# Winograd convolution on one core: the store of image 10 is cut into three transfers, two of them over 100 and 28 channels

## The chip, the cores and the metric

The kernel runs on one NeuronCore of a Trainium2 chip. The core has five engines: PE (TensorE, matrix multiply), DVE (VectorE), ACT (ScalarE), POOL (GpSimd) and SP (SyncE, which here only issues transfers). Data moves between device memory (HBM) and the on-chip memory (SBUF) by 16 DMA engines, which all queues share. A transfer is issued by an engine's queue: SP's transfers appear in the profile as queue q1, ACT's as q10, POOL's as q0; q8 and q14 carry the program's own instructions. A packet is one contiguous piece that one DMA engine moves.

The metric is device time in microseconds (us) of one execution. Three runs of the kernel before took 126.14, 126.81 and 127.47 us; the median is 126.81 us.

## What is computed

A 3x3 convolution with a border of zeros: 16 images of 64 channels and 64x64 pixels, 128 output channels, all float32.

```
for b, co, ci, kh, kw:
    output[b, co] += weight[co, ci, kh, kw] * x_pad[b, ci, kh:kh+h, kw:kw+w]
```

The input is 16.8 MB (1 MB an image), the output 33.6 MB (2 MB an image).

## The kernel before

Two images make a pair (`NP = 8` pairs, index `p` from 0 to 7), because 64 channels of two images fill the 128 partitions of SBUF. The convolution is done as a one-dimensional Winograd transform over rows: two neighbouring output rows share a product. For a block of 16 output rows (`blk` 0 to 3), `group` (L114 to L149) runs three sets of matmuls into PSUM: `U` on the sum of two input rows (`ss`), `A` for the even output rows, `Bt` for the odd ones. ACT copies `U` to SBUF (`ut`, L155), and DVE adds it to `A` (L164) and to `Bt` (L167), which leaves the finished rows in `ot`, one tile of 128 output channels (the partitions) by 64 rows by 64 columns for each image. A channel of an image is 16 KB, contiguous in SBUF and in HBM.

Input comes in three ways. The weights and the first two pairs are loaded by SP as float32 (L42, L46, L48); pairs 2 to 7 are loaded by POOL with a cast to float16 (`load`, L58). POOL also adds up the row sums `ss` of later pairs (L67).

Output is what the change touches. `store` (L96 to L100) issues one transfer of the rows `lo` to `hi` of all 128 channels. After the last block of a pair, SP stores the first image of the pair (L171), as soon as DVE's last addition to it is done; the second image is put into the list `held`, and ACT issues it in the next block, after its `ut` copies (L160 to L161). For pairs 0 to 6 a store is a whole image, 2 MB; in pair 7 each image is stored as two halves of 32 rows (L168). The tiles of images 10 to 15 (pairs 5 to 7) are not used again, so nothing in the program waits for their stores but the program's end (L200, SP).

There is one more order that the change touches. Transfers from SP and ACT take the semaphores that tell of their landing in turn, from eight: the ninth such transfer has the semaphore of the first, and its queue waits until the first has landed before it issues the ninth. In the order of the program, these transfers are the weights (1), the three loads (2 to 4), and the stores of pair 0 (5 and 6), and so on to the four stores of pair 7 (19 to 22). The store of image 10, which the change cuts, is number 15.

Of the kernel before, what the change touches and what calls it, by code (L numbers as in the profile page):

```python
# [13 lines left out]
def kernel(  # L14
# [6 lines left out]
    nc = tc.nc  # L21
    B, CI, H, W = x.shape
    CO = weight.shape[0]
    assert H == 64 and W == 64 and CI == 64 and CO == 128 and B % 2 == 0
    NP = B // 2
# [4 lines left out]
    out_rows = out.rearrange("b co h w -> b co h w")  # L30
# [25 lines left out]
    def load(p):  # L56
        xs[p] = xpool.tile([128, H, W], F16, tag="xs", name="xs")
        keep(nc.gpsimd.dma_start(xs[p], x_rows[128 * p : 128 * p + 128, :, :]))  # L58
# [3 lines left out]
    def sums(eng, p, src, lo, n):  # L62
        if p not in ss:
            ss[p] = spool.tile([128, H // 2, W], F16, tag="ss", name="ss")
        v = src.rearrange("p (j i) c -> p j i c", i=2)
        keep(
            eng.tensor_add(  # L67
                ss[p][:, lo : lo + n, :], v[:, lo : lo + n, 0, :], v[:, lo : lo + n, 1, :]
            )
        )  # L70
# [22 lines left out]

    held = []

    def store(eng, p, b2, ot, lo, hi):  # L96
        return eng.dma_start(
            out_rows[2 * p + b2, :, lo:hi, :],
            ot.rearrange("p j i c -> p (j i) c")[:, lo:hi, :],
        )  # L100

    for p in range(NP):
        if p + 1 < NP:
            for lo in (0, 16):
                sums(nc.gpsimd, p + 1, x1 if p == 0 else xs[p + 1], lo, 16)
        if p > 0 and p + 4 < NP:
            load(p + 4)
        ots = [
            opool.tile([128, H // 2, 2, W], F32, tag="ot", name="ot") for _ in range(2)
        ]  # L110
        for blk in range(4):
            j0 = blk * RB

            def group(wi_rows):  # L114

                tiles = [
                    psum.tile([128, RB, W], F32, tag="acc", name="acc") for _ in range(2)
                ]
                n = 3 * len(wi_rows)
                i = 0  # L120
                for wi, off in wi_rows:
                    for kw in (1, 0, 2):
                        c_lo, c_hi = max(0, 1 - kw), min(W, W + 1 - kw)
                        for b2 in range(2):
                            p0 = 64 * b2
                            lo, hi = j0, j0 + RB
                            if off is None:
                                rhs = ss[p][p0 : p0 + 64, lo:hi, c_lo + kw - 1 : c_hi + kw - 1]
                            else:
                                while 2 * lo + off < 0:  # L130
                                    lo += 1
                                while 2 * (hi - 1) + off > H - 1:
                                    hi -= 1
                                first = 2 * lo + off
                                last = 2 * (hi - 1) + off
                                rhs = xs[p][
                                    p0 : p0 + 64,
                                    first : last + 1 : 2,
                                    c_lo + kw - 1 : c_hi + kw - 1,
                                ]  # L140
                            nc.tensor.matmul(  # L141
                                tiles[b2][:, lo - j0 : hi - j0, c_lo:c_hi],
                                Wt[p0 : p0 + 64, wi, kw, :],
                                rhs,
                                start=i == 0,
                                stop=i == n - 1,
                            )
                        i += 1
                return tiles  # L149

            U = group([(G1, None)])
            us = []
            for b2 in range(2):
                ut = upool.tile([128, RB, W], F32, tag="ut", name="ut")
                keep(nc.scalar.copy(ut, U[b2]))  # L155
                us.append(ut)
            if p == 0:
                for lo in {2: (0, 16), 3: (32, 48)}.get(blk, ()):
                    keep(nc.scalar.copy(xs[1][:, lo : lo + 16, :], x1[:, lo : lo + 16, :]))  # L159
            while held:  # L160
                keep(store(nc.scalar, *held.pop(0)))  # L161
            A = group([(G21, 1), (G0, -1)])
            for b2 in range(2):
                nc.vector.tensor_add(ots[b2][:, j0 : j0 + RB, 0, :], A[b2], us[b2])  # L164
            Bt = group([(G01, 0), (G2, 2)])
            for b2 in range(2):
                nc.vector.tensor_add(ots[b2][:, j0 : j0 + RB, 1, :], Bt[b2], us[b2])  # L167
            parts = {3: (0, 64)} if p < NP - 1 else {1: (0, 32), 3: (32, 64)}  # L168
            if blk in parts:
                lo, hi = parts[blk]  # L170
                store(nc.sync, p, 0, ots[0], lo, hi)  # L171
                held.append((p, 1, ots[1], lo, hi))
    while held:
        keep(store(nc.scalar, *held.pop(0)))
# [30 lines left out]
```

## Time and profile before

| what | value |
|---|---|
| median of three runs | 126.81 us |
| the profiled execution's own time | 126.72 us |
| its span, first to last instruction | 124.9 us |
| mean granted clock of PE | 0.968 |
| busy: PE, DVE, ACT, POOL | 106.7, 82.6, 44.4, 36.9 us |
| moved by DMA | 44.48 MB in 4042 packets, mean 356 GB/s |
| store of 2 MB, from issue to landing (SP, ACT) | 20.1, 19.8 us |
| issue of one store on SP | 0.33 us |

The span is what the profile covers; 1.8 us of the execution's time lie outside it. "Busy" is the time in which an engine executes, added up. The DMA share of a stretch is the mean over the 16 DMA engines, so that 1.00 means that all sixteen move data all the time; it is counted where a packet begins, so a short stretch can show more than 1.00. "From issue to landing" contains the time that a transfer stands behind others in the queues.

### The profile page before, as it was taken

The page shows a single profiled execution, that of the slowest core. Times are in us where ns is not written, and L with a number is a line of the kernel's source. Part 1 is how long each engine was busy: PE and PEld are TensorE (multiplying, and loading weights), DVE is VectorE, ACT ScalarE, POOL GpSimd, SP SyncE. Part 2 cuts the span into 40 slices and gives each one's busy share as a digit, 9 for nine tenths or more (in the row PEclk, how much of TensorE's full clock was granted, in tenths as well). Part 3 has the DMA queues.
Part 4 walks back from the last instruction along what each step waited for, and adds up shares of the span by engine and source line. Part 5 has one row for each costly group of instructions (what it writes and reads, how often), then busy time and mean ns, then how long its engine had stood idle before and what let it go on. Part 6 is the DMA issues. An engine that isn't in the chain of part 4 may idle for free.

```text
span 124.9 us, 2407 instructions
## 1 busy us (share of the span) xinstructions
PE 106.7 (85%) x978; PEld 55.9 (45%) x978; DVE 82.6 (66%) x132; ACT 44.4 (36%) x76; POOL 36.9 (30%) x29
## 2 busy tenths in 40 slices
PE   0489999999999999999999999999999999990000
PEld 0334455555555555555555555555555555540000
DVE  0106897877787778788788878777877787772000
ACT  4439569633333333333333333333333333330000
POOL 2391059997059001760008500093000000000000
PEclk9999999999999999999999999999999999999755
DMA  4999999999999999999999999999999999999991
GB/s 127 341 429 409 289 220 220 210 254 357 386 344 354 328 375 359 367 338 344 386 359 354 338 344 401 428 435 441 414 430 430 425 420 435 435 420 407 430 391 66
DMA packets 4042, 44.48 MB, mean 356 GB/s; under 512 B 448, under 2 KB 448, under 8 KB 704
## 3 DMA queue, kind: packets, MB, share of 16 engines
q1 hardware_dynamic: 1872, 21.27, 41.2%
q10 hardware_dynamic: 1296, 16.78, 31.7%
q0 software_dynamic: 864, 6.29, 24.4%
q8 instruction: 7, 0.11, 0.3%
q14 instruction: 3, 0.02, 0.0%
HBM read 17.07 MB, written 33.55 MB: 405 GB/s over the span
## 4 chain that ended last, share of the span: by engine, by line
PE 78%; DMA 6%; ACT 3%; DVE 1%; SPq 1%; issue 1%; DVEq 0%
PE acc L141 78%; DMA x<-in_x_dram 6%; ACT xs L92 2%; ACT ut L155 1%; DVE ot L164 1%; DVE ot L167 0%; DVEq L200 0%; SPq L46 0%; SPq L42 0%; DVEq L164 0%
## 5 line engine op out<-in xcount | busy, mean ns | idle before, releaser
L141 PE MATMUL acc<-xs,Wt 64*128 64x504 f16 (+3 forms) x768 | 94.8, 378 | 0.2
L141 PEld LDWEIGHTS <-Wt 64*128 64x128 f16 x960 | 54.7, 96 | 51.6 <-issue 4.2
L155 ACT COPY ut<-acc 128x512 f32<-128x512 f32 x64 | 34.3, 589 | 60.3 <-issue 40.6
L164 DVE TENSOR_TENSOR ot<-acc,ut 128x512 f32<-128x512 f32 x64 | 41.2, 686 | 21.9 <-PE acc L141 18.0
L167 DVE TENSOR_TENSOR ot<-acc,ut 128x512 f32<-128x512 f32 x64 | 41.1, 684 | 0.0
L141 PE MATMUL acc<-ss,Wt 64*128 64x504 f16 (+1 forms) x192 | 32.5, 384 | 1.0 <-DVE ss L67 1.0
L67 POOL TENSOR_TENSOR ss<-xs 128x1024 f16<-128x1024 f16 x12 | 25.2, 2126 | 23.6 <-DMA xs<-in_x_dram 12.5
L67 DVE TENSOR_TENSOR ss<-x 128x512 f16<-128x512 f32 x4 | 2.6, 689 | 8.8 <-DMA x<-in_x_dram 8.8
L58 POOL DMA_DIRECT2D xs<-in_x_dram x6 | 3.5, 578 | 13.3 <-PE acc L141 13.3
L67 POOL TENSOR_TENSOR ss<-x 128x1024 f16<-128x1024 f32 x2 | 4.7, 2360 | 7.1 <-DMA x<-in_x_dram 7.1
L84 PE MATMUL wp<-ident,w 128*64 128x128 f16 x18 | 1.3, 328 | 4.3 <-POOL w L52 4.3
L92 ACT CAST xs<-x 128x1024 f16<-128x1024 f32 (+2 forms) x4 | 4.0, 1048 | 2.3 <-DMA x<-in_x_dram 2.3
L159 ACT CAST xs<-x 128x1024 f16<-128x1024 f32 x4 | 4.0, 1058 | 0.0
L84 PEld LDWEIGHTS <-w 128*64 128x64 f16 x18 | 1.1, 210 | 4.2 <-POOL w L52 4.2
L85 ACT CAST Wt<-wp 128x384 f16<-128x384 f32 x3 | 1.2, 487 | 2.9 <-PE wp L84 2.9
L86 POOL TENSOR_TENSOR Wt<-Wt 128x384 f16<-128x384 f16 x1 | 1.5, 1460 | 1.7 <-ACT Wt L85 1.7
L85 ACT ACT_TABLE_LOAD x1 | 1.3, 1283 | 0.7 <-PEq L189 0.7
L52 POOL CAST w<-w_raw 128x576 f16<-128x576 f32 x1 | 0.7, 663 | 2.2 <-DMA w_raw<-in_weight_dram 2.2
L87 POOL TENSOR_TENSOR Wt<-Wt 128x384 f16<-128x384 f16 x1 | 0.9, 902 | 0.0
masks.py:199 POOL TENSOR_SCALAR_AFFINE_SELECT ident<-ident 128x128 f16<-128x128 f16 x1 | 0.3, 292 | 0.1
masks.py:197 POOL MEMSET ident<- 128x128 f16 x1 | 0.2, 205 | 0.3 <-POOLq L189 0.3
L189 POOL MEMSET const-float32-0.0<- 128x1 f32 x1 | 0.1, 98 | 0.2 <-issue 0.2
(3 smaller groups left out, 0.3 us busy)
## 6 DMA issues: line engine op xcount, KB each, us to landing
out_dram<-ot SPq DMA_DIRECT2D x7, 2048.0 KB, 20.1
out_dram<-ot ACTq DMA_DIRECT2D x7, 2048.0 KB, 19.8
xs<-in_x_dram POOLq DMA_DIRECT2D x6, 1024.0 KB, 25.9
x<-in_x_dram SPq DMA_DIRECT2D x1, 2048.0 KB, 14.8
out_dram<-ot SPq DMA_DIRECT2D x2, 1024.0 KB, 11.6
out_dram<-ot ACTq DMA_DIRECT2D x2, 1024.0 KB, 11.5
x<-in_x_dram SPq DMA_DIRECT2D x1, 1472.0 KB, 7.9
x<-in_x_dram SPq DMA_DIRECT2D x1, 576.0 KB, 4.7
```

The costliest lines, as they stand in the source:

```text
L58: keep(nc.gpsimd.dma_start(xs[p], x_rows[128 * p : 128 * p + 128, :, :]))
L67: eng.tensor_add(ss[p][:, lo : lo + n, :], v[:, lo : lo + n, 0, :], v[:, lo : lo + n, 1, :])
L84: nc.tensor.matmul(wp[q : q + 64, k * CO : k * CO + CO], w16[:, t::9], ident)
L85: keep(nc.scalar.copy(wrow(g), wp[:, 0 : 3 * CO]))
L86: keep(nc.gpsimd.tensor_sub(wrow(G21), wrow(G2), wrow(G1)))
L87: keep(nc.gpsimd.tensor_sub(wrow(G01), wrow(G0), wrow(G1)))
L92: keep(nc.scalar.copy(xs[0][:, lo:hi, :], x0[:, lo:hi, :]))
L141: nc.tensor.matmul(tiles[b2][:, lo - j0 : hi - j0, c_lo:c_hi], Wt[p0 : p0 + 64, wi, kw, :], rhs, start=i == 0, stop=i == n - 1,)
L155: keep(nc.scalar.copy(ut, U[b2]))
L159: keep(nc.scalar.copy(xs[1][:, lo : lo + 16, :], x1[:, lo : lo + 16, :]))
L164: nc.vector.tensor_add(ots[b2][:, j0 : j0 + RB, 0, :], A[b2], us[b2])
L167: nc.vector.tensor_add(ots[b2][:, j0 : j0 + RB, 1, :], Bt[b2], us[b2])
```

## The change

For `p == NP - 3`, which is pair 5, the store of the first image (image 10) is issued as three transfers on SP in place of one. The first takes rows 0 to 53 of all 128 channels. The second takes rows 54 to 63 of channels 0 to 99, the third the same rows of channels 100 to 127. Together they write the same bytes. The stores of the other images, the second image of pair 5 among them, stay as they are. `store` gets two more arguments, the bounds of the channels.

```diff
-    def store(eng, p, b2, ot, lo, hi):
+    def store(eng, p, b2, ot, lo, hi, c_lo=0, c_hi=CO):
         return eng.dma_start(
-            out_rows[2 * p + b2, :, lo:hi, :],
-            ot.rearrange("p j i c -> p (j i) c")[:, lo:hi, :],
+            out_rows[2 * p + b2, c_lo:c_hi, lo:hi, :],
+            ot.rearrange("p j i c -> p (j i) c")[c_lo:c_hi, lo:hi, :],
         )
...
             if blk in parts:
                 lo, hi = parts[blk]
-                store(nc.sync, p, 0, ots[0], lo, hi)
+                if p == NP - 3:
+                    store(nc.sync, p, 0, ots[0], lo, 54)
+                    store(nc.sync, p, 0, ots[0], 54, hi, 0, 100)
+                    store(nc.sync, p, 0, ots[0], 54, hi, 100, CO)
+                else:
+                    store(nc.sync, p, 0, ots[0], lo, hi)
                 held.append((p, 1, ots[1], lo, hi))
```

## Prediction

> **What bounds the kernel now.** I first read the table of DMA queues, because PE at 85% of the span leaves room for another bound.
>
> ```profile
> q1 hardware_dynamic: 1872, 21.27, 41.2%
> q10 hardware_dynamic: 1296, 16.78, 31.7%
> q0 software_dynamic: 864, 6.29, 24.4%
> q8 instruction: 7, 0.11, 0.3%
> ```
>
> The last column is each queue's time as a share of sixteen engines' span. The sum is 97.6% of 124.9 us: on average each DMA engine moves data for 121.9 us. The rest is the start (the first transfer is issued at 0.73 us) and the end. DMA is the bound, more than PE. The table also shows how a store is dealt out: q10 carries ACT's nine stores, and 1296 / 9 = 144 packets = 16 x (8 + 1): eight channels and one semaphore write for each of 16 engines.
>
> Next, stretches of the span, with the DMA share and GB/s in the last two columns.
>
> ```profile
> 12.50:75.00 62.50, 62.31 (x583) 32.66 (x581) 49.95 (x80) 25.66 (x46) 27.31 (x15) 1.00 1.02 326
> 75.00:113.00 38.00, 37.16 (x349) 19.39 (x343) 29.75 (x48) 12.16 (x23) 4.20 (x2) 1.00 1.01 426
> 113.00:121.00 8.00, 0.00 (x0) 0.00 (x0) 0.34 (x1) 0.00 (x0) 0.00 (x0) 0.75 1.00 424
> 121.00:124.90 3.90, 0.00 (x0) 0.00 (x0) 0.00 (x0) 0.00 (x0) 0.00 (x0) 0.50 0.27 113
> ```
>
> From 12.5 to 121 us all sixteen engines are full; after 113 us nothing computes. So what one engine has to do more or less in the middle is still there at its end. The waits of SP's queue agree: it waits for DVE before each store, and at the end 10.6 us for stores.
>
> ```profile
> SPq L97 <- DVE ot L167: 107.0, 9, 20.6
> SPq L200 <- DMA out_dram<-ot: 10.6, 6, 4.2
> ```
>
> The end itself, in quarters of a microsecond:
>
> ```profile
> 121.00:121.25 0.25, 0.00 (x0) 0.00 (x0) 0.00 (x0) 0.00 (x0) 0.00 (x0) 0.50 0.78 328
> 121.50:121.75 0.25, 0.00 (x0) 0.00 (x0) 0.00 (x0) 0.00 (x0) 0.00 (x0) 0.50 0.55 229
> ...
> 122.25:122.50 0.25, 0.00 (x0) 0.00 (x0) 0.00 (x0) 0.00 (x0) 0.00 (x0) 0.50 0.40 164
> 122.50:122.75 0.25, 0.00 (x0) 0.00 (x0) 0.00 (x0) 0.00 (x0) 0.00 (x0) 0.50 0.32 131
> 122.75:123.00 0.25, 0.00 (x0) 0.00 (x0) 0.00 (x0) 0.00 (x0) 0.00 (x0) 0.50 0.09 33
> 123.00:123.25 0.25, 0.00 (x0) 0.00 (x0) 0.00 (x0) 0.00 (x0) 0.00 (x0) 0.50 0.16 66
> 123.25:123.50 0.25, 0.00 (x0) 0.00 (x0) 0.00 (x0) 0.00 (x0) 0.00 (x0) 0.50 0.00 0
> ```
>
> The engines don't end together. 66 GB/s for 0.25 us are two packets of 8 KB: two engines are still at work after 123 us, while others stopped before 121.5. The packet records give each engine's end, since in the full stretch a packet begins 3 or 4 ns before the one ahead of it on its engine ends, and so the packets link into sixteen chains. They end (us) at 120.9, 121.2, 121.2, 121.3, 121.4, 121.6, 121.7; then 122.4, 122.6, 122.6, 122.7, 122.8, 122.8, 122.9; then 123.3 and 123.5. The seven instruction packets of q8 (0.88 to 0.96 us each, and some 0.4 us on the packet behind) lie in seven different chains, all of the later nine. The last chain has none; between 77 and 114 us its 16 KB packets take 0.63 to 0.66 us, where the others' take 0.61. **The program ends when the slowest of sixteen DMA engines ends.** The trace doesn't number the engines.
>
> **The change, part by part.** *Packets.* In the full stretch a 16,384 B packet takes 611 ns and an 8,192 B one 309 ns: 8192 / 302 = 27.1 B/ns and 7 ns fixed. So 54 rows (13,824 B) take 517 ns and ten rows (2,560 B) 101 ns. A semaphore write takes 9 ns. Before, image 10 costs each engine 8 x 611 + 9 = 4,897 ns.
>
> *How 100 and 28 channels are dealt out* no row shows, since every transfer here has 128. One bound is sixteen even shares, as in all rows: 8 x (517 + 101) + 27 = 4,971, +0.07 us on each engine. The far bound is one engine for both pieces: 128 x 101 = 12.9 us on it, some +12 us. Nearest to the rows, where each engine has the same whole number of channels, is the largest number of engines up to 16 that divides the channels: 10 engines with 10 channels, and 14 engines with 2. I take that, with the ten among the fourteen. Then:
> - ten engines: 8 x 517 + 12 x 101 + 27 = 5,375, **+0.48 us**
> - four engines: 8 x 517 + 2 x 101 + 18 = 4,356, **-0.54 us**
> - two engines: 8 x 517 + 9 = 4,145, **-0.75 us**
>
> The Trainium skill ("DMA: Bandwidth & Descriptors", in the section on why a DMA increments its semaphore by 16 and not by 1) gives the same division, 100 partitions on 10 engines, the lowest-numbered ones; no run here shows it yet. The same page's rules for kernel authors speak against the change: to use all 16 engines, the outermost dimension should be a multiple of 16, which 100 and 28 are not.
>
> *Does the shift reach the end?* An engine must not run dry behind it. Image 10's store is issued at 87.16 us and lands at 104.1; the next store on the queue comes at 99.97 and lands at 113.6, the one after at 106.3. Work is always queued, so each engine's end moves by its own sum.
>
> *Issues.* SP issues two more transfers.
>
> ```profile
> L97 SPq DMA_DIRECT2D out_dram<-ot x9: 332/333/348, 23.1 to 112.8; - x9
> L97 SPq EVENT_SEMAPHORE  x7: 17/17/17, 36.3 to 106.7; - x7
> ```
>
> That is 2 x 0.33 us and two semaphore waits of 17 ns, on SP at 87.5 us, with nothing queued behind until 99.97: nothing. ACT's store of image 11 (87.76 us) may overlap SP's third issue; if it had to wait out 0.33 us, ACT's next `ut` copy, which comes after some 2 us of idle time, hides it, and the DMA engines are full anyway.
>
> *Semaphores.* The eight are taken in turn, and the two new transfers (16 and 17) push each later one two places on. Number 16 needs number 8 (landed 58.0 us), 17 needs 9 (72.5), 18 needs 10 (72.7); pair 6 needs 11 and 12 (84.8), the first half of pair 7 needs 13 and 14 (94.7). The last two stores (issued at 112.8 and 113.4) now need parts of image 10, which land near 104.6: 8 us to spare. No wait binds. At the end SP waits for the semaphores in fixed order, about 60 ns a step. Before, the last landing (123.95 us) is followed by two more steps; after, the last store has the last semaphore of that order. **-0.12 us**.
>
> *The sum* depends on where the latest engines fall. Without a number on the chains, the last one is among the ten with a chance of 10/16: +0.48 - 0.12 = **+0.36 us**. On the profiled execution's 126.72 (124.9 span and 1.8 around it) that is 127.08; it lies 0.09 under the runs' median of 126.81, so 127.2 on that. I say 127.1.
>
> The skill's same page (section on latency and other measured facts) says that engines 7 and 15 are usually the slow ones, by its guess from descriptor traffic of POOL's transfers. Here one engine is slow from 77 us on, when POOL's last load is nearly done (it lands at 81.0), until 114, so the guess doesn't fit, but the numbers may: were it 7, the sum is the one above, were it 15, that engine ends at 122.7 and another is last.
>
> **Rivals.** All are counted at the 85% that I give to the 10-and-14 division, unless said.
> - *The last engine is among the six, the second last among the ten* (6/16 x 10/15): 123.32 + 0.48 = 123.80 against 123.47, +0.33 - 0.12 = +0.21: 126.9 us. Speaking for it: 0.15 us alone part the two.
> - *Both are among the six* (6/16 x 5/15): then an engine with an instruction packet is last, 122.9 + 0.48 = 123.38, -0.09 - 0.12 = -0.2: 126.5 us, faster. It can't be much more: the lightest of the nine late engines ends at 122.4, at least three of the nine are among the ten, so the end is at least 122.6 + 0.48 = 123.1, -0.5 with the semaphores: 126.2 us.
> - *The change doesn't shift load* (sixteen even shares or nearly): +0.07 - 0.12, 126.7 us, no change. For it: every row of the trace is even.
> - *The spread is narrower*, for example a power of two that divides both 100 and 28, which is four engines: 8 x 517 + 32 x 101 + 27 = 7,395, +2.5 us on four and -0.75 on the others. It costs over 1% as soon as one of the four ended after 122.2 before, as nine of sixteen did (1 - (7x6x5x4)/(16x15x14x13) = 98%): about 122.9 + 2.5 = 125.4, +1.8: 128.6 us, slower. Against it: nothing in the trace uses fewer than 16.
> - *Faster by over 1%* would need more than an even finish of all engines. The mean of the sixteen ends is 122.1; 123.47 less this is 1.4 us, 1.1%, and only three sizes of shift are to be had.
>
> **How the numbers follow.** 1%, about what a measurement here can tell from no change, is 1.27 us. Chances: last engine among the ten 0.53; second last 0.21; both among the six 0.11; no shift 0.07; narrower spread 0.06; faster for a cause I don't see 0.02. The first four lie between -0.5 and +0.4 us, within 1%. The runs before scatter by 0.7 us around their median, so a small true shift can pass 1% either way; I move 0.04 to slower, where most of it points, and 0.03 to faster. Faster 0.05, same 0.85, slower 0.10. For the range I take the cases' 126.5 to 127.2 and add half a microsecond of scatter: 126.0 to 127.7; the narrow spread stays outside.
>
> **What will show it.** q1 should have 1872 - 144 + 144 + 110 + 42 = 2024 packets (data and semaphores; 2032 if all sixteen engines take part in each piece, 2008 if four do), and in the quarter-microsecond stretches the end should show ten engines later and six earlier. The last packet begins near 123.6 us where it began at 123.15. Wrong would be: a store after 99 us issued later than DVE releases it (a semaphore wait), a DMA share under 0.95 between 90 and 120 us, or a slow engine that is another one in each execution, which would make the chances mere averages over runs.

## The result, and the profile after

The changed kernel takes 127.16 us (median of 22 runs), the one before 126.66 us (22 runs beside them). The ratio is 1.0035, with a 95% interval of 1.0019 to 1.0050: a little slower, by the ratio +0.44 us (0.24 to 0.63). The forecast was no change beyond 1%, with +0.36 us as the likeliest sum.

The profiled execution of after took 127.14 us with a span of 125.4 us. Its page, the table of DMA queues (packets, MB, share of sixteen engines' span):

```profile
q1 hardware_dynamic: 2024, 21.27, 41.1%
q10 hardware_dynamic: 1296, 16.78, 31.5%
q0 software_dynamic: 864, 6.29, 24.3%
q8 instruction: 7, 0.11, 0.3%
```

q1 moves the same bytes in 2024 packets, the number that goes with ten engines for 100 channels and fourteen for 28. Long stretches of after, with DMA share and GB/s at the end of a line:

```profile
75.00:113.00 38.00, 37.24 (x350) 31.90 (x345) 29.72 (x49) 12.35 (x24) 4.21 (x2) 1.00 1.01 426
113.00:121.00 8.00, 0.00 (x0) 0.00 (x0) 0.53 (x1) 0.00 (x0) 0.00 (x0) 0.62 1.00 424
121.00:125.40 4.40, 0.00 (x0) 0.00 (x0) 0.00 (x0) 0.00 (x0) 0.00 (x0) 0.50 0.25 102
```

From 75 to 121 us the DMA engines are as full as before, with the same GB/s. The weight loads of PE (PEld, the second busy time of a line, 31.90 us) appear longer than before (19.39), but e3 below has 19.49 and is slower still, so that is not where time goes. The difference lies in the last line, which is half a microsecond longer. In quarters of a microsecond, after:

```profile
121.50:121.75 0.25, 0.00 (x0) 0.00 (x0) 0.00 (x0) 0.00 (x0) 0.00 (x0) 0.50 0.86 361
...
122.00:122.25 0.25, 0.00 (x0) 0.00 (x0) 0.00 (x0) 0.00 (x0) 0.00 (x0) 0.50 0.24 98
122.25:122.50 0.25, 0.00 (x0) 0.00 (x0) 0.00 (x0) 0.00 (x0) 0.00 (x0) 0.50 0.23 98
122.50:122.75 0.25, 0.00 (x0) 0.00 (x0) 0.00 (x0) 0.00 (x0) 0.00 (x0) 0.50 0.31 131
122.75:123.00 0.25, 0.00 (x0) 0.00 (x0) 0.00 (x0) 0.00 (x0) 0.00 (x0) 0.50 0.08 33
123.00:123.25 0.25, 0.00 (x0) 0.00 (x0) 0.00 (x0) 0.00 (x0) 0.00 (x0) 0.50 0.08 33
123.25:123.50 0.25, 0.00 (x0) 0.00 (x0) 0.00 (x0) 0.00 (x0) 0.00 (x0) 0.50 0.08 33
123.50:123.75 0.25, 0.00 (x0) 0.00 (x0) 0.00 (x0) 0.00 (x0) 0.00 (x0) 0.50 0.00 0
```

At 121.50 more engines are at work than before (0.86 against 0.55): those that ended early now end later. From 122.75 on, one packet begins in a quarter: a single engine, which ends 0.8 us later than any other.

The packet records, linked end to start as in the prediction, show which. In after each chain also tells its class, by its packets of 2,560 B: 12, 2 or none.

```
                    ends before (us)                          ends after (us)
ten (12 packets)    not told apart                            121.5 121.7 121.8 121.9 121.9 122.1
                                                              122.6 122.8 123.0 | slow one: 123.8
four (2 packets)                                              122.0 122.1 122.1 122.8
two (none)                                                    120.7 121.9
all                 120.9 121.2 121.2 121.3 121.4 121.6 121.7
                    122.4 122.6 122.6 122.7 122.8 122.8 122.9
                    123.3 | slow one: 123.5
```

The slow engine, known by 49 packets of 16 KB at 0.63 us or more between 76 and 113 us, has 12 small packets. It is one of the ten, and it ends 0.35 us later than before. Its packets of image 10 take 5,687 ns in place of 5,204: +0.48 us, the shift that the sum has for one of the ten. Its chain was 0.07 us ahead at 83 us already, and its other packets took 0.05 us less.

The waits of SP's queue in after:

```profile
SPq L97 <- DVE ot L167: 104.9, 9, 20.8
SPq L205 <- DMA out_dram<-ot: 10.4, 3, 4.7
```

Every store still waits for DVE alone; no wait for a semaphore's earlier transfer has come in.

### The profile page after: what moved, and what is told of

Read it like the earlier page. It is cut to its first block, busy times and chain, and to the rows that moved or that the text cites. A ratio compares the mean times of both kernels' runs of the same rounds, so it can differ in the third digit from the quotient of the medians.

```text
span 125.4 us, 2409 instructions
## 1 busy us (share of the span) xinstructions
PE 106.9 (85%) x978; PEld 89.4 (71%) x978; DVE 82.7 (66%) x132; ACT 44.4 (35%) x76; POOL 36.8 (29%) x29
## 3 DMA queue, kind: packets, MB, share of 16 engines
q1 hardware_dynamic: 2024, 21.27, 41.1%
## 4 chain that ended last, share of the span: by engine, by line
PE 83%; DMA 4%; DVE 2%; issue 1%; DVEq 0%; SPq 0%
PE acc L141 83%; DMA x<-in_x_dram 4%; DVE ot L164 1%; DVE ss L67 1%; DVE ot L167 0%; DVEq L205 0%; SPq L42 0%
## 5 line engine op out<-in xcount | busy, mean ns | idle before, releaser
L141 PEld LDWEIGHTS <-Wt 64*128 64x128 f16 x960 | 88.2, 96 | 18.0 <-issue 4.2
L141 PE MATMUL acc<-xs,Wt 64*128 64x504 f16 (+3 forms) x768 | 92.0, 380 | 0.0
L141 PE MATMUL acc<-ss,Wt 64*128 64x504 f16 (+1 forms) x192 | 29.3, 384 | 1.0 <-DVE ss L67 1.0
```

The source lines that it names most:

```text
L141: nc.tensor.matmul(tiles[b2][:, lo - j0 : hi - j0, c_lo:c_hi], Wt[p0 : p0 + 64, wi, kw, :], rhs, start=i == 0, stop=i == n - 1,)
```

## Experiments

Each is an edit of the changed kernel, in the three calls of `store` for pair 5, and still writes the whole output. The times beside them are of the kernel before on the same chip.

### e1: cut in rows alone

```diff
-                    store(nc.sync, p, 0, ots[0], 54, hi, 0, 100)
-                    store(nc.sync, p, 0, ots[0], 54, hi, 100, CO)
+                    store(nc.sync, p, 0, ots[0], 54, 64)
```

> Image 10 in two transfers, rows 0 to 53 and rows 54 to 63, both of all 128 channels: cut in rows, not in channels. Theory (the slowest DMA engine ends the program and the 100 and 28 channels load ten engines more): each engine has the same share, 8 x (516 + 102) + 18 = 4962 ns against 4897, +0.07 us; the last store has the seventh of the eight semaphores in SP's final order, one step of 0.06 us less: together 0.0 us, 126.7 us. Rival (cutting the store and issuing more transfers costs the time, whatever the channels): half or more of the change's +0.5 us, 126.9 to 127.2 us.

Measured: 126.64 us (12 runs), before 126.64 (23 runs); ratio 0.9997 (0.9981 to 1.0013), between -0.24 and +0.16 us. Cutting the store in rows costs nothing that can be measured, and packets of 2,560 B alone don't either; what is left is the cut in channels. SP's stores in e1 (min/median/max duration in ns) show that a long issue costs nothing either:

```profile
L97 SPq DMA_DIRECT2D out_dram<-ot x10: 332/332/1540, 23.1 to 112.8; - x10
```

### e2: the same three transfers, a fifth of the bytes

```diff
-                    store(nc.sync, p, 0, ots[0], lo, 54)
-                    store(nc.sync, p, 0, ots[0], 54, hi, 0, 100)
-                    store(nc.sync, p, 0, ots[0], 54, hi, 100, CO)
+                    store(nc.sync, p, 0, ots[0], 0, 62)
+                    store(nc.sync, p, 0, ots[0], 62, 64, 0, 100)
+                    store(nc.sync, p, 0, ots[0], 62, 64, 100, 128)
```

> The same three transfers as the change, but over rows 0 to 61 and 62 to 63: the same issues, semaphores and channel counts, a fifth of the bytes shifted. Theory: on the ten engines 8 x 593 + 12 x 26 + 27 = 5083 ns, +0.19 us, less 0.12 us of semaphore steps: +0.07 us, 126.7 us. Rival (the long issues on SP, 1.4 and 0.7 us, or the semaphores in turn, cost the time): the whole +0.5 us of the change, 127.2 us.

Measured: 126.76 us (12 runs), before 126.64; ratio 1.0012 (0.9991 to 1.0034), +0.15 us (-0.11 to +0.43). The rival's +0.5 us is outside, but the lower end of what was measured for the change (+0.24) is not: by itself e2 is weak evidence against it. Nor were the issues quite the same: the two that are added took 0.82 and 0.70 us here, 1.39 and 0.67 us in after.

### e3: the same three transfers, 2.4 times the bytes

```diff
-                    store(nc.sync, p, 0, ots[0], lo, 54)
-                    store(nc.sync, p, 0, ots[0], 54, hi, 0, 100)
-                    store(nc.sync, p, 0, ots[0], 54, hi, 100, CO)
+                    store(nc.sync, p, 0, ots[0], 0, 40)
+                    store(nc.sync, p, 0, ots[0], 40, 64, 0, 100)
+                    store(nc.sync, p, 0, ots[0], 40, 64, 100, 128)
```

> The same three transfers over rows 0 to 39 and 40 to 63: 2.4 times the bytes shifted. Theory: on the ten engines 8 x 385 + 12 x 234 + 27 = 5915 ns against 4897, +1.02 us, less 0.12: +0.9 us, 127.6 us; in the packet chains the engine that ends last is one of the ten. Rival (issues or semaphores): as the change, +0.5 us, 127.2 us.

Measured: 127.67 us (5 runs), before 126.64; ratio 1.0088 (1.0070 to 1.0106), +1.11 us (0.89 to 1.34). The theory's +0.9 lies at the lower end of the interval, the rival's +0.5 far outside. The cost follows the bytes: +0.15, +0.44, +1.11 us for 2, 10 and 24 rows, where the sum gives +0.07, +0.36, +0.90. One thing moved besides: rows 0 to 39 are finished a block earlier, and SP issues them at 83.9 us in place of 87.2, while the queues are full (DMA share 1.00 from 75 to 113 us). The end of e3:

```profile
122.50:122.75 0.25, 0.00 (x0) 0.00 (x0) 0.00 (x0) 0.00 (x0) 0.00 (x0) 0.50 0.39 164
...
123.50:123.75 0.25, 0.00 (x0) 0.00 (x0) 0.00 (x0) 0.00 (x0) 0.00 (x0) 0.50 0.16 66
123.75:124.00 0.25, 0.00 (x0) 0.00 (x0) 0.00 (x0) 0.00 (x0) 0.00 (x0) 0.50 0.08 33
124.00:124.25 0.25, 0.00 (x0) 0.00 (x0) 0.00 (x0) 0.00 (x0) 0.00 (x0) 0.50 0.08 33
124.25:124.50 0.25, 0.00 (x0) 0.00 (x0) 0.00 (x0) 0.00 (x0) 0.00 (x0) 0.50 0.00 0
```

The trail is a microsecond longer than before's. The chain that ends last (124.5 us) is the slow one, with 12 small packets. The two issues that are added took 0.35 and 0.33 us here, shorter together than in after, e1, e2, e7 and e8, in the kernel that is slowest.

### e4, e5 and e6: numbering the engines

Pieces of few channels give each engine a count of small packets that tells its number, if a piece always takes the lowest engines. The number is thus a place in that order. The edit of e4:

```diff
-                    store(nc.sync, p, 0, ots[0], lo, 54)
-                    store(nc.sync, p, 0, ots[0], 54, hi, 0, 100)
-                    store(nc.sync, p, 0, ots[0], 54, hi, 100, CO)
+                    store(nc.sync, p, 0, ots[0], 0, 62)
+                    store(nc.sync, p, 0, ots[0], 62, 64, 0, 112)
+                    store(nc.sync, p, 0, ots[0], 62, 64, 112, 120)
+                    store(nc.sync, p, 0, ots[0], 62, 64, 120, 127)
+                    store(nc.sync, p, 0, ots[0], 62, 64, 127, 128)
```

e5 has rows 60 to 63 and the bounds 0, 112, 119, 123, 126, 128; e6 the same rows and 0, 112, 118, 123, 127, 128.

> A look that numbers the DMA engines: rows 62 and 63 of image 10 go out as pieces of 112, 8, 7 and 1 channels. If a piece goes to the largest number of engines up to 16 that divides its channels, always from the lowest on, then beside the 7 small packets of the first piece engine 0 has three more, engines 1 to 6 two, engine 7 one, engines 8 to 15 none. Theory A (the slow engine is number 7): its chain has 8 small packets. Theory B (it is a lower one): 9 or 10. Theory C (8 or 9): 7. The time is of no interest; by the sums some 126.9 us.

> Rows 60 to 63 of image 10 go out as pieces of 112, 7, 4, 3 and 2 channels. Beside the 7 packets of 1024 B of the first piece, engines 0 and 1 then have four more, engine 2 three, engine 3 two, engines 4 to 6 one, engines 7 to 15 none. The look before put the slow engine among 1 to 6, but its packets of 512 B followed each other so closely that chains may have been exchanged. Theory B (it is one of 1 to 6): its chain has 8 to 11 small packets here. Theory A (number 7): 7. The time is of no interest.

> As the look before, with pieces of 112, 6, 5, 4 and 1 channels: engine 0 has four more small packets, engines 1 to 3 three, engine 4 two, engine 5 one, engines 6 to 15 none. Theory B: the count agrees with the look before on one engine from 1 to 6. Theory A: 7 small packets. The time is of no interest.

Counted: the slow chain has 9 small packets in e4 (engines 1 to 6), 8 in e5 (4 to 6) and 9 in e6 (engine 4). All three agree on **engine 4**. In e5 the linking exchanges the slow chain for another at 100 us; the part behind it, with the slow packets that follow, is the one counted, and its small packets too are slow (47 to 59 ns against 46). The single runs of e4, e5 and e6 took 127.01, 127.14 and 127.12 us (before: 126.64, median of 23, for e4 and 127.11, one run, for e5 and e6), which says nothing on the cost.

The order of the semaphores, which holds up no store in after, shows here. With four transfers more than before (e4), SP's queue waits for earlier stores to land:

```profile
SPq L97 <- DMA out_dram<-ot: 6.9, 2, 3.6
```

No later store goes out late for it in e4. With five more, in e5 and e6 (8.9 and 6.2 us of such waits), the last piece is issued at 94.05 and 93.94 us, 5 and 3 us behind the one ahead of it, and ACT's next store at 103.85 and 103.82 us, where it was 100.57 before. The DMA engines stay full even so (DMA share 1.00 or 1.01 from 75 to 113 us).

In the same way as the slow engine, the seven instruction packets fall, by their times, on engines 10 to 13 (19, 33, 46 and 61 us), 14 or 15 (74), 5 (87) and 6 (101). Engine 1 has one packet of q14, engine 3 two. The rest end early.

### e7 and e8: another set of engines

If the end belongs to an engine and not to the cut, then loading engines that end early should cost nothing, up to a point. 123 channels are 3 x 41. The edit of e7:

```diff
-                    store(nc.sync, p, 0, ots[0], lo, 54)
-                    store(nc.sync, p, 0, ots[0], 54, hi, 0, 100)
-                    store(nc.sync, p, 0, ots[0], 54, hi, 100, CO)
+                    store(nc.sync, p, 0, ots[0], 0, 60)
+                    store(nc.sync, p, 0, ots[0], 60, 64, 0, 123)
+                    store(nc.sync, p, 0, ots[0], 60, 64, 123, 128)
```

e8 is the same with row 56 for row 60.

> The counting puts the slow engine at number 4, engines 0 and 2 among those that end early and engine 1 a little later (ends of 121.2, 121.3 and 121.6 us before). Rows 60 to 63 of image 10 go out as 123 channels (3 x 41, so on engines 0 to 2) and 5 channels (engines 0 to 4). Theory: engines 0 to 2 get 8 x 573 + 42 x 46 + 27 = 6543 ns against 4897, +1.65 us; the slow one 8 x 573 + 46 + 18 = 4648, -0.25; engines 5 to 15 -0.30. The slow engine ends at 123.2 us, engine 1 at 123.25: -0.2 us, and 0.12 less for the semaphores' order: -0.3 us, 126.3 us, faster than before. Rival (any cut over fewer than 128 channels costs time, as in the change): +0.4 us or more, 127.1 us.

> The same over rows 56 to 63: twice the bytes on engines 0 to 2. Theory: these get 8 x 535 + 42 x 82 + 27 = 7751 ns, +2.85 us, and engine 1 ends at 124.5 us in place of the slow one, which ends at 122.95: +1.0 - 0.12 = +0.9 us, 127.5 us; the chain that ends last has 42 small packets. Rival (the slow engine ends the program whatever the others carry): -0.5 - 0.12 = -0.6 us, 126.0 us.

Measured: e7 126.56 us, before 126.71; ratio 0.9993 (0.9975 to 1.0011), -0.09 us (-0.32 to +0.14): no difference that can be told, where -0.3 us was expected and +0.4 by the rival. The rival is out; the expected gain lies at the edge of the interval, so that it was not seen, and not quite excluded. The chains of its profiled execution, at 126.25 us the second fastest of twelve, are close to the sum: the slow engine, with one small packet, ends at 123.07, the three loaded ones at 122.62, 122.88 and 122.98, and one with an instruction packet at 122.94. With three engines within 0.2 us of the last, small differences between executions are likely to decide which is last, and the latest of several is later than the sum for one; this was not shown apart. Where many packets of like length meet (e3, e7, e8), chains can be exchanged in the linking, so there the ends are surer than whose they are.

e8 takes 127.43 us, before 126.71; ratio 1.0060 (1.0039 to 1.0081), +0.76 us (0.49 to 1.03), with +0.9 expected and -0.6 by the rival. Its end, in halves of a microsecond:

```profile
122.50:123.00 0.50, 0.00 (x0) 0.00 (x0) 0.00 (x0) 0.00 (x0) 0.00 (x0) 0.50 0.24 98
123.00:123.50 0.50, 0.00 (x0) 0.00 (x0) 0.00 (x0) 0.00 (x0) 0.00 (x0) 0.50 0.23 98
123.50:124.00 0.50, 0.00 (x0) 0.00 (x0) 0.00 (x0) 0.00 (x0) 0.00 (x0) 0.50 0.08 33
```

The three chains with 42 small packets are the last now, at 123.69, 123.99 and 124.03 us, while the slow engine ends at 122.56. So the end was moved, as intended, from engine 4 to engines 0 to 2. No version was found that measurably beats the kernel before: e7 can't be told from it.

## Why the prediction held, step by step

- **DMA is the bound and the slowest engine ends the program.** Held: e1, e3 and e8 follow it in size and sign, and e2 agrees with it, though its interval takes in zero. The one forecast that wasn't met is the gain of e7, -0.3 us expected and -0.09 (-0.32 to +0.14) measured.
- **Packet times.** 517 and 101 ns were worked out; 516 and 102 ns are the usual ones in after.
- **Ten, fourteen, sixteen engines.** Held: 2024 packets, and chains with 12, 2 and no small packets. This was the choice between bounds 12 us apart. The Trainium skill's rule ("DMA: Bandwidth & Descriptors", section on why a DMA increments its semaphore by 16 and not by 1) agrees with these counts: 100 channels on 10 engines, and the piece of 28 takes in the same ten.
- **The shift reaches the end.** Held: the DMA share stays at 1.00 to 121 us. The early engines of the ten end at 121.5 to 122.1 us, where their like ended at 120.9 to 121.7. The slow one moved by 0.35 us and not 0.48, though its packets of image 10 took 0.48 us more. One execution of each can't show the end of an engine to a tenth: in e1, where the sum gives +0.07, the slow one ends at 123.09 us, 0.38 earlier than before.
- **The last engine is among the ten.** This was a chance of 10/16 that came true, and to that extent the sum was lucky: nothing in the trace before told the class of the slow engine. The skill's same page (section on latency and other measured facts) has engines 7 and 15 as the usual slow ones; here the counts give engine 4, and engine 7 ends early.
- **Issues on SP.** Mis-sized: 0.33 us was set for each of the two, and they took 1.39 and 0.67 us. They cost nothing all the same, as e1 shows with 1.54 us: SP has nothing else to issue until 100 us.
- **Semaphores.** No wait came in, as worked out. That both pieces on SP would take their semaphores ahead of ACT's store was wrong in a detail: by the landings that each semaphore counts, ACT's store took number 16, behind the first piece, and the two others 17 and 18. The end is as said: from the last landing to SP's last step it was 0.94 us before (123.93 to 124.87; the prediction's 123.95 is SP's step behind the landing) and is 0.83 us after (124.47 to 125.30), 0.11 us less for the two steps that are gone.
- **The sum.** +0.36 us against a measured +0.44 (0.24 to 0.63). The last data packet begins at 123.50 us, where 123.6 was forecast.

Of the rivals, even shares and a narrower spread fall with the packet counts, and those with the slow engine among the six with its chain. The bound for "faster by over 1%" was slightly misread: the sixteen ends average 122.17 us and not 122.1, so an even finish would be worth 1.3 us, 1.0%, just the limit.

## What to carry to other kernels

Here the DMA engines are full to the end, and the time is that of the one engine that ends last, not of the mean: link the packets, and see what each engine has to do. In these traces a store over a number of channels that 16 doesn't divide went to fewer engines, the smaller set always among the larger, so a cut of a few rows shifts work among engines, for better or worse; know which engine is last before cutting. Such shifts are small (here some 0.05 us for each row that is cut into 100 and 28 channels), and the end before shows how little one can gain: the next engine ends 0.15 us ahead of the last.

## What was not expected of the hardware

- One engine, number 4 by the counts, moves most of its 16 KB packets in 0.63 to 0.67 us in place of 0.61 from about 76 us to 113 us, when computing ends and its packets become 8 KB ones, in every trace here. Its 8 KB packets from 114 us on take 0.31 us, as the others' do. It ends last in all of them but e8, where others carry more, and e4, where a chain with 7 small packets ends at 123.47 us and the slow one at 123.28; in e1 it is last by 0.03 us alone. Why it is slow is open.
- The program's own instruction packets matter: seven of 16 KB, each on a different engine, put that engine some 1.3 us behind those without.
- The time of an issue on SP was 0.33 to 1.54 us for transfers of much the same kind: 1.54 us for ten rows of 128 channels (e1), 0.35 us for 24 rows of 100 (e3), 1.39 us for ten rows of 100 (after). Neither channels nor the place behind another issue explains it (e8 has 0.36 us directly behind one); no time followed from it.
